# HGRN2 scan on one Trainium2 core: block totals kept at the blocks' first positions, and the epsilon of the norms added by ScalarE

## The chip, the cores and the metric

The kernel runs on one core of a Trainium2 chip. The metric is the device time of one execution in microseconds (us). The engines are TensorE (PE; its weight loads are a queue of their own, PEld), VectorE (DVE), ScalarE (ACT), GpSimd (POOL) and SyncE (SP, which issues most transfers).

## The reference

One layer of a decoder, everything float32, with T = 1024 positions and D = 1024 channels: an HGRN2 mixer of 8 heads of 128 channels, then an MLP of 4096 hidden channels, and a norm at the end. Cut to what is computed:

```
h = rmsnorm(x) * gain
q, f, i, g = split(h @ w_in, 4)                    # w_in: 1024 x 4096
log_f = log(lb + (1 - lb) * sigmoid(f));  k = (1 - lb) * sigmoid(-f);  q = silu(q) * 128**-0.5
# in each head:  S_t = diag(f_t) S_{t-1} + k_t v_t^T ;  o_t = S_t^T q_t     (v = i)
o = o * rsqrt(mean(o*o) + 1e-6) * out_norm * silu(g)
x = x + o @ w_out
x = x + relu(rmsnorm(x) @ w1)**2 @ w2
out = rmsnorm(x)
```

## The kernel before

Each float32 operand of a large product is split into a high part, which ACT copies (L162 for the weights of the input projection, L782 for the output projection), and a low part, which DVE makes by subtraction (L163, L783); each product is three passes on TensorE (L209 to L211). The input projection of a head is two "pairs", one for q and f, one for v and g, and each of them is computed from seven products of half-size blocks named a, b, s2, s1, s3, s4, d in place of eight. The weight sums that s1 to s4 need are made on DVE (L145, tiles raw). So w5s1, w5s3, w5s4 and so on are split operands of pair 5, whose products belong to head 2; pair 2h and pair 2h+1 belong to head h, and while they are computed the recurrence of head h-1 runs beside them.

The recurrence works by levels. Within a chunk of 128 positions, blocks of 1, 2, 4, 8, 16, 32 and 64 positions are joined in twos. At each size m, the scores between the odd block's q and the even block's k are one set of small matmuls; then the level is closed: carry_q multiplies the odd block's q by the total of f over the even block, carry_k multiplies the even block's k by the total of the odd block, and carry_f multiplies the two totals into the total of the joined block. All three are products on DVE (L392, L399, L405). The total of a block is a column of the tile f itself; before the change it stands at the block's last position (column m - 1).

The levels are spread over steps, which a list at the end of scan_units gives for each head:

- prefixes, before the matmuls: q times f, the level-1 product of q, and the tile qd, which holds q as the diagonal and sizes 1 and 2 see it.
- small: matmuls of k with qd (L568), then carry_k, carry_f of size 1 and all three of size 2, then prefixes_2, and eight masked copies of the scores into the tile Ac (L579 to L583).
- prefixes_2: the product of q at size 4 and the tile qe (L590, ACT; L594, ACT; L595, DVE), which holds q as sizes 4 and 8 see it.
- middle: matmuls of k with qe (L601), then carry_k and carry_f of size 4, all three of size 8, and three masked copies (L610).
- leaf(16): matmuls of k and q of size 16 (L619), the level's three products, a masked copy (L622), and four copies of ACT from Ac into AT (L626).
- big(32) and big(64): matmuls (L649), ACT's copies into AT (L652), the three products; at size 64 the total goes to the tile tot.
- kt, vt, kv: transposes of k and v and the states' updates (L664 to L693).
- o_unit: the output o (L706, L708), its sums of squares on ACT (L712), then rstd_of; z_unit: z = o times rs_z on ACT (L718); zt: z's transposes on TensorE (L755).

rstd_of makes 1/sqrt(ss + eps): an addition and a power with exponent -0.5, both on POOL (L114, L115). It is called for z of each head (128 x 8), for the eight row tiles of the norm ahead of the MLP (rs_n), and for rows of the final norm (rs_f).

The order on TensorE is written by hand: the steps are put into the projection's matmuls at fixed distances (SPACING, 1730 ns of matmul time). The order on DVE, ACT, POOL and SP is written by hand only at the start of the program and again from the output projection on; within the scan a scheduler chooses it, from the order of the code, the readiness of operands and the buffers.

Of the kernel before, what the change touches and what calls it, by code (L numbers as in the profile page):

```python
# [29 lines left out]
P = 128  # L30
# [19 lines left out]
def trunk(ctx: ExitStack, tc: tile.TileContext, x, gains, masks, gfin, w_in, w_out, w1, w2, out):  # L50
# [60 lines left out]

    def rstd_of(ss, eps, width, tag):
        r = pool.tile([P, width], F32, name=f"rs_{tag}", tag=f"rs{width}", bufs=8 if width == 1 else 2)
        nc.gpsimd.tensor_scalar(r, ss, eps, None, op0=ALU.add)  # L114
        nc.gpsimd.tensor_tensor(r, r, neghalf[:, :width], ALU.pow)  # L115
        return r

# [131 lines left out]
    with tc.tile_pool(name="scan", bufs=1) as sp:  # L249
# [137 lines left out]
        def carry_q(q, f, m):  # L387

            n = T // (2 * m)
            te = halves(f, m)[:, :, 0, m - 1:m]  # L390
            qo = halves(q, m)[:, :, 1, :]
            nc.vector.tensor_tensor(qo, qo, te.to_broadcast([P, n, m]), ALU.mult)  # L392

        def carry_k(k, f, m):

            n = T // (2 * m)
            to = halves(f, m)[:, :, 1, m - 1:m]
            ke = halves(k, m)[:, :, 0, :]
            nc.vector.tensor_tensor(ke, ke, to.to_broadcast([P, n, m]), ALU.mult)  # L399

        def carry_f(f, m):

            fv = halves(f, m)
            te, to = fv[:, :, 0, m - 1:m], fv[:, :, 1, m - 1:m]
            nc.vector.tensor_tensor(to, te, to, ALU.mult)  # L405

        shapes = {"q": ([P, T], 2), "qd": ([P, T // LEAF, 80], 1), "k": ([P, T], 1), "f": ([P, T], 1),
                  "vT": ([P, T], 1), "sg": ([P, T], 1)}
# [128 lines left out]
        def prefixes(tl):  # L537


            q, f, qd = tl["q"], tl["f"], tl["qd"]  # L540
            qb = q.rearrange("p (n l) -> p n l", l=LEAF)
            nc.vector.tensor_tensor(qb, qd[:, :, :LEAF], f.rearrange("p (n l) -> p n l", l=LEAF), ALU.mult)
            nc.scalar.activation(qd[:, :, 32:48], qb[:, :, 1::2], AF.Copy)
            carry_q(q, f, 1)
            q4 = q.rearrange("p (n b j) -> p n b j", b=8, j=4)
            f4 = f.rearrange("p (n b j) -> p n b j", b=8, j=4)
            x1 = qd[:, :, 48:64].rearrange("p n (b j) -> p n b j", j=2)
            x0 = qd[:, :, 64:80].rearrange("p n (b j) -> p n b j", j=2)
            nc.scalar.activation(x1, q4[:, :, :, 2:4], AF.Copy)
            nc.vector.tensor_tensor(x0, q4[:, :, :, 2:4], f4[:, :, :, 1:2].to_broadcast([P, 32, 8, 2]), ALU.mult)  # L550

        def scan_units(h, tl):

# [6 lines left out]
            def small():  # L560
                pss = []
                for g in range(2):
                    ps = psum.tile([P, 4, 80], F32, name=f"lv{h}_0_{g}", tag="s")
                    pss.append(ps)
                    for j in range(4):
                        for b in range(P // LEAF):
                            n = (4 * g + j) * 4 + b
                            nc.tensor.matmul(ps[b * LEAF:(b + 1) * LEAF, j, :], k[:, n * LEAF:(n + 1) * LEAF],  # L568
                                             tl["qd"][:, n, :], start=True, stop=True)
                carry_k(k, f, 1)  # L570
                carry_f(f, 1)
                carry(2)
                prefixes_2()
                m0, m1, m2, m3 = (mk[:, i:i + 1, :] for i in range(4))
                m2, m3 = (m.rearrange("p c (b j) -> p c b j", j=4) for m in (m2, m3))
                for g, ps in enumerate(pss):
                    ac = Ac[:, 4 * g:4 * g + 4, :]
                    a4 = ac.rearrange("p c (b j) -> p c b j", j=4)
                    nc.vector.copy_predicated(ac, m0.to_broadcast([P, 4, LEAF]), ps[:, :, :LEAF])  # L579
                    nc.vector.copy_predicated(ac[:, :, 1::2], m1[:, :, 1::2].to_broadcast([P, 4, 16]), ps[:, :, 32:48])  # L580
                    for i, mm in enumerate((m2, m3)):
                        pv = ps[:, :, 48 + 16 * i:64 + 16 * i].rearrange("p c (b j) -> p c b j", j=2)
                        nc.vector.copy_predicated(a4[:, :, :, 2:4], mm[:, :, :, 2:4].to_broadcast([P, 4, 8, 2]), pv)  # L583

            def prefixes_2():
# [6 lines left out]
                q16, f16 = (a.rearrange("p (n b j) -> p n b j", b=2, j=16) for a in (q, f))  # L592
                x1, x0 = (qe[:, :, c:c + 16].rearrange("p n (b j) -> p n b j", j=8) for c in (16, 32))
                nc.scalar.activation(x1, q16[:, :, :, 8:16], AF.Copy)  # L594
                nc.vector.tensor_tensor(x0, q16[:, :, :, 8:16], f16[:, :, :, 7:8].to_broadcast([P, 32, 2, 8]), ALU.mult)  # L595

            def middle():
                ps = psum.tile([P, NC, 48], F32, name=f"lv{h}_4", tag="s")
# [2 lines left out]
                    nc.tensor.matmul(ps[b * LEAF:(b + 1) * LEAF, c, :], k[:, n * LEAF:(n + 1) * LEAF],  # L601
                                     st["qe"][:, n, :48], start=True, stop=True)
                carry_k(k, f, 4)
                carry_f(f, 4)
                carry(8)
                for i, j, lo in ((4, 4, 0), (5, 8, 16), (6, 8, 32)):
                    odd = [a.rearrange("p c (b two j) -> p c b two j", two=2, j=j)[:, :, :, 1, :]
                           for a in (Ac, mk[:, i:i + 1, :])]
# [20 lines left out]
            def carry(m):  # L629

                carry_q(q, f, m)
                carry_k(k, f, m)
                if m == 64:
                    tot = st["tot"] = sp.tile([P, NC], F32, name=f"tot{h}", tag="tot", bufs=2)
                    fv = halves(f, m)
                    nc.vector.tensor_tensor(tot, fv[:, :, 0, m - 1], fv[:, :, 1, m - 1], ALU.mult)
                else:
                    carry_f(f, m)

# [743 lines left out]
```

## Time and profile before

| | |
|---|---|
| median of 3 runs | 1139.62 us (1139.31 to 1140.0) |
| the profiled execution | 1139.92 us |
| its span | 1138.1 us |
| TensorE busy | 1126.3 us, 99% of the span |
| VectorE busy | 831.2 us, 73% |
| ScalarE busy | 593.8 us, 52% |
| GpSimd busy | 40.6 us, 4% |

The span runs from the first to the last instruction of the profiled execution; 1.8 us of the execution's time lie outside it. The scan's eight heads lie between about 50 us and 470 us, some 51 us each; the output projection, the MLP and the final norm follow to 1131 us, and the last 7 us are the final rows' norm and their way out. In a row of a timeline the first number is the start, the second the time from the start to the end of the group of like instructions (xN is how many), and brackets name how long the engine was idle before and what ended that. On DVE and ACT, an instruction's row reaches a little into the next one's.

### The profile page before, as it was taken

To read this page: it belongs to the slowest core of one execution; us is meant where nothing else is said; L and a number is where in the kernel's file an instruction comes from. 1 tells how busy PE (TensorE), PEld (TensorE's weight loads), DVE (VectorE), ACT (ScalarE), POOL (GpSimd) and SP (SyncE) were. 2 spreads that over 40 slices of the span, in tenths; PEclk is the share of its full clock that TensorE was granted. 3 is DMA by queue.
4 is the path that set the end of the run, shared out by engine and by line. 5 is a ranking of instruction groups with operands and counts; after the bars stand their busy time and mean duration, and the time that the engine had idled before them with its cause. 6 is when DMAs were issued, how large, how long until landed. Compare 5 with 4: busy or idle time off the path is not lost.

```text
span 1138.1 us, 17625 instructions
## 1 busy us (share of the span) xinstructions
PE 1126.3 (99%) x7052; PEld 931.2 (82%) x7052; DVE 831.2 (73%) x1208; ACT 593.8 (52%) x1036; POOL 40.6 (4%) x68
## 2 busy tenths in 40 slices
PE   9999999999999999999999999999999999999997
PEld 7778888887878778888888888888888888888886
DVE  6897888878787889677855664565498755777674
ACT  7756556464645575456664544454553443323552
POOL 1000000000000000010000000000000000000011
PEclk9999999999999999999999999999999999999999
DMA  6113132312223176412244522452798635323331
GB/s 264 38 39 133 62 122 76 112 57 93 75 76 126 55 263 205 150 74 75 93 190 180 203 120 103 185 204 108 259 364 299 206 113 220 113 93 97 126 129 75
DMA packets 48466, 158.58 MB, mean 139 GB/s; under 512 B 5504, under 2 KB 5632, under 8 KB 48384
## 3 DMA queue, kind: packets, MB, share of 16 engines
q1 hardware_dynamic: 47520, 156.26, 38.4%
q8 instruction: 55, 0.90, 0.3%
q10 hardware_dynamic: 864, 1.20, 0.3%
q14 instruction: 27, 0.22, 0.1%
HBM read 109.99 MB, written 47.45 MB: 138 GB/s over the span
## 4 chain that ended last, share of the span: by engine, by line
PE 88%; DVE 5%; ACT 2%; DMA 2%; issue 1%; POOL 1%; POOLq 0%; ACTq 0%; DVEq 0%
PE m1X L210 5%; PE m1X L211 5%; PE m1X L209 5%; PE m2X L209 5%; PE m2X L211 5%; PE m2X L210 5%; PE pX L209 4%; PE pX L211 3%; PE pX L210 3%; PE m1Y L210 3%; PE m2Y L209 3%; PE m1Y L211 3%; PE m1Y L209 3%; PE m2Y L211 3%; PE m2Y L210 3%; PE pY L209 2%
## 5 line engine op out<-in xcount | busy, mean ns | idle before, releaser
L993 ACT ACTIVATE a<-ai 128x1024 fp32r<-128x1024 f32 x56 | 58.9, 1052 | 71.4 <-PE m2X L210 28.3
L994 DVE TENSOR_TENSOR a<-ai,a 128x1024 fp32r<-128x1024 f32 x56 | 68.3, 1219 | 11.1 <-ACT a L993 11.1
L1095 ACT ACTIVATE e<-e 128x1024 f32<-128x1024 f32 x24 | 25.5, 1062 | 72.5 <-DVE e L1142 72.5
L1172 DVE TENSOR_TENSOR acc<-acc,m2X 128x512 f32<-128x512 f32 x32 | 21.1, 685 | 34.3 <-PE m2X L211 34.2
L392 DVE TENSOR_TENSOR q<-q,f 128x512 f32<-128x512 f32 x56 | 38.4, 687 | 2.2 <-PE lv L649 2.2
L399 DVE TENSOR_TENSOR k<-k,f 128x512 f32<-128x512 f32 x56 | 38.3, 684 | 0.0
L1092 ACT ACTIVATE e<-e 128x1024 f32<-128x1024 f32 x32 | 34.0, 1062 | 1.0
L626 ACT ACTIVATE AT<-Ac 32x256 f32<-32x256 f32 x32 | 13.3, 415 | 35.3 <-DVE Ac L622 35.1
L145 DVE TENSOR_TENSOR raw<-raw,raw 128x512 f32<-128x512 f32 x42 | 29.0, 689 | 0.8
L718 ACT ACTIVATE z<-o,rs_z 128x128 f32<-128x128 f32 x64 | 17.4, 384 | 17.8 <-POOL rs_z L115 17.8
L1123 ACT ACTIVATE e<-m1X 128x512 f32<-128x512 f32 x30 | 16.9, 593 | 17.2 <-PE m1X L211 17.2
L706 PE MATMUL o<-v,AT 128*128 128x128 f32 x128 | 23.4, 275 | 0.0
L114 POOL TENSOR_SCALAR rs_f<-fs 128x1 f32<-128x1 f32 x4 | 2.1, 531 | 570.5 <-ACT ot L1176 570.5
L1172 DVE TENSOR_TENSOR acc<-acc,m2Y 128x512 f32<-128x512 f32 x16 | 10.8, 686 | 15.4 <-PE m2Y L211 14.7
L708 PE MATMUL o<-S,q 128*128 128x128 f32 x112 | 21.7, 275 | 0.0
L1142 DVE TENSOR_TENSOR e<-e,m1Y 128x512 f32<-128x512 f32 x16 | 10.9, 686 | 14.2 <-PE m1Y L211 14.2
L706 PEld LDWEIGHTS o<-v,AT 128*128 128x128 f32 x128 | 19.4, 191 | 0.6
L405 DVE TENSOR_TENSOR f<-f 128x512 f32<-128x512 f32 (+5 forms) x48 | 19.0, 396 | 0.1
L693 DVE SCALAR_TENSOR_TENSOR S<-S,tot,kv 128x128 f32<-128x128 f32 x48 | 16.7, 347 | 2.0
L114 POOL TENSOR_SCALAR rs_z<-zs 128x8 f32<-128x8 f32 x8 | 3.7, 458 | 390.1 <-ACT z L712 390.1
L708 PEld LDWEIGHTS o<-S,q 128*128 128x128 f32 x112 | 17.0, 192 | 0.0
L712 ACT ACTIVATE z<-o 128x128 f32<-128x128 f32 x64 | 16.7, 284 | 0.1
(1843 smaller groups left out, 3886.4 us busy)
## 6 DMA issues: line engine op xcount, KB each, us to landing
raw<-in_w_in SPq DMA_DIRECT2D x32, 512.0 KB, 3.6
ai<-adt SPq DMA_DIRECT2D x32, 512.0 KB, 4.4
adB<-e SPq DMA_DIRECT2D x24, 512.0 KB, 2.6
adt<-t SPq DMA_DIRECT2D x24, 512.0 KB, 4.3
ai<-adB SPq DMA_DIRECT2D x24, 512.0 KB, 4.5
izs<-sd SPq DMA_DIRECT2D x21, 256.0 KB, 3.3
x<-in_x SPq DMA_DIRECT2D x8, 512.0 KB, 7.1
xr<-in_x SPq DMA_DIRECT2D x8, 512.0 KB, 5.5
```

The costliest lines, as they stand in the source:

```text
L145: nc.vector.tensor_tensor(out_, a, b, ALU.add)
L209: nc.tensor.matmul(ps, lhi, rhi, start=start, stop=False, **more)
L210: nc.tensor.matmul(ps, lhi, rlo, start=False, stop=False, **more)
L211: nc.tensor.matmul(ps, llo, rhi, start=False, stop=stop, **more)
L392: nc.vector.tensor_tensor(qo, qo, te.to_broadcast([P, n, m]), ALU.mult)
L399: nc.vector.tensor_tensor(ke, ke, to.to_broadcast([P, n, m]), ALU.mult)
L706: nc.tensor.matmul(ps[:, j, :], AT[:, c, :], v[:, c, :], start=True, stop=c == 0)
L708: nc.tensor.matmul(ps[:, j, :], q[:, c * P:(c + 1) * P], st["S"][:, c - 1, :], start=False, stop=True)
L993: nc.scalar.activation(hi, x, AF.Copy)
L994: nc.vector.tensor_tensor(lo, x, hi.bitcast(F32), ALU.subtract)
L1092: nc.scalar.activation(t, t, AF.Square)
L1172: nc.vector.tensor_tensor(t, t, ps, op)
```

## The change

- **Where totals stand.** carry_f writes the joined total to the first position of the even block rather than the last of the odd one, and all readers take it from there. carry_k reads the odd block's total, which carry_f of the same size no longer overwrites; so carry_f of a size need not wait for carry_k of that size, nor carry_k of one size stand between the totals of this and the next.
- **What is written where.** carry_f(1), carry_q(2), carry_f(2) move from small, behind its matmuls, into prefixes, ahead of them. carry_f(4), carry_q(8), carry_f(8) move from middle into prefixes_2. In small and middle only carry_k remains.
- **Epsilon.** In rstd_of the addition is an ACT activation (Copy with a bias) instead of a POOL tensor_scalar. The power stays on POOL. There are 20 such additions: 8 for rs_z, 8 for rs_n, 4 for rs_f.

The diff (line numbers behind the additions shift by 3 to 4):

```diff
     def rstd_of(ss, eps, width, tag):
...
-        nc.gpsimd.tensor_scalar(r, ss, eps, None, op0=ALU.add)
+        nc.scalar.activation(r, ss, AF.Copy, bias=eps)
         nc.gpsimd.tensor_tensor(r, r, neghalf[:, :width], ALU.pow)
...
         def carry_q(q, f, m):
-            te = halves(f, m)[:, :, 0, m - 1:m]
+            te = halves(f, m)[:, :, 0, 0:1]
...
         def carry_k(k, f, m):
-            to = halves(f, m)[:, :, 1, m - 1:m]
+            to = halves(f, m)[:, :, 1, 0:1]
...
         def carry_f(f, m):
-            te, to = fv[:, :, 0, m - 1:m], fv[:, :, 1, m - 1:m]
-            nc.vector.tensor_tensor(to, te, to, ALU.mult)
+            te, to = fv[:, :, 0, 0:1], fv[:, :, 1, 0:1]
+            nc.vector.tensor_tensor(te, te, to, ALU.mult)
...
         def prefixes(tl):
...
+            carry_f(f, 1)
+            carry_q(q, f, 2)
+            carry_f(f, 2)
...
             def small():
...
                 carry_k(k, f, 1)
-                carry_f(f, 1)
-                carry(2)
+                carry_k(k, f, 2)
                 prefixes_2()
...
             def prefixes_2():
...
+                carry_f(f, 4)
+                carry_q(q, f, 8)
+                carry_f(f, 8)
...
             def middle():
...
                 carry_k(k, f, 4)
-                carry_f(f, 4)
-                carry(8)
+                carry_k(k, f, 8)
```

On TensorE the order is the same, instruction by instruction. What moves elsewhere is shown at three places of head 1.

VectorE, head 1, from k of size 1, behind the size-1 and size-2 matmuls, to qe. In the names, q1, k1, f1 are the head's tiles, lv1_0_0 and lv1_0_1 the matmuls' results, and the shape tells the size (128x256x2 is size 2). Before:

```order
L399 TENSOR_TENSOR k1_991<-k1_991,f1_992 128x512
L583 COPY_PREDICATED Ac_153<-mk_74,lv1_0_0_1249 128x32x2
L405 TENSOR_TENSOR f1_992<-f1_992 128x512
L579 COPY_PREDICATED Ac_153<-mk_74,lv1_0_1_1266 128x128
L392 TENSOR_TENSOR q1_825<-q1_825,f1_992 128x256x2
L399 TENSOR_TENSOR k1_991<-k1_991,f1_992 128x256x2
L580 COPY_PREDICATED Ac_153<-mk_74,lv1_0_1_1266 128x64
L405 TENSOR_TENSOR f1_992<-f1_992 128x256
L583 COPY_PREDICATED Ac_153<-mk_74,lv1_0_1_1266 128x32x2
L392 TENSOR_TENSOR q1_825<-q1_825,f1_992 128x128x4
L583 COPY_PREDICATED Ac_153<-mk_74,lv1_0_1_1266 128x32x2
L595 TENSOR_TENSOR qe1_1288<-q1_825,f1_992 128x32x16
```

The same place now, where f of size 1, q and f of size 2 stand ahead of the matmuls, and three of the masked copies behind qe (L597 now):

```order
L399 TENSOR_TENSOR k1_991<-k1_991,f1_992 128x512
L585 COPY_PREDICATED Ac_153<-mk_74,lv1_0_0_1252 128x32x2
L399 TENSOR_TENSOR k1_991<-k1_991,f1_992 128x256x2
L392 TENSOR_TENSOR q1_825<-q1_825,f1_992 128x128x4
L581 COPY_PREDICATED Ac_153<-mk_74,lv1_0_1_1269 128x128
L597 TENSOR_TENSOR qe1_1288<-q1_825,f1_992 128x32x16
L405 TENSOR_TENSOR f1_992<-f1_992 128x128
L582 COPY_PREDICATED Ac_153<-mk_74,lv1_0_1_1269 128x64
```

The stretch from the first k to qe has twelve rows before and six now; f of size 4 follows qe at once.

VectorE, head 1, from q of size 16 to k of size 32; raw50 and w5s1, w5s3 are weights of pair 5. Before:

```order
L392 TENSOR_TENSOR q1_825<-q1_825,f1_992 128x32x16
L399 TENSOR_TENSOR k1_991<-k1_991,f1_992 128x32x16
L622 COPY_PREDICATED Ac_153<-mk_74,lv1_16_1403 128x256
L405 TENSOR_TENSOR f1_992<-f1_992 128x32
L145 TENSOR_TENSOR raw50_1135<-raw50_1135 128x512
L145 TENSOR_TENSOR raw50_1135<-raw50_1135,raw51_1136 128x512
L392 TENSOR_TENSOR q1_825<-q1_825,f1_992 128x16x32
L399 TENSOR_TENSOR k1_991<-k1_991,f1_992 128x16x32
```

Now:

```order
L392 TENSOR_TENSOR q1_825<-q1_825,f1_992 128x32x16
L399 TENSOR_TENSOR k1_991<-k1_991,f1_992 128x32x16
L405 TENSOR_TENSOR f1_992<-f1_992 128x32
L626 COPY_PREDICATED Ac_153<-mk_74,lv1_16_1403 128x256
L163 TENSOR_TENSOR w5s1_1526<-raw50_1138,w5s1_1526 128x512
L145 TENSOR_TENSOR raw50_1138<-raw50_1138,raw51_1139 128x512
L163 TENSOR_TENSOR w5s3_1591<-raw50_1138,w5s3_1591 128x512
L392 TENSOR_TENSOR q1_825<-q1_825,f1_992 128x16x32
L399 TENSOR_TENSOR k1_991<-k1_991,f1_992 128x16x32
```

Between the masked copy into Ac and q of size 32 (128x16x32) there were two weight sums and a short product of f; now there are a sum and the splits of w5s1 and w5s3. In head 2 the order is the same with w7; in heads 3 to 6 q and k of size 32 stand ahead of the second split; in head 7 six splits of the output projection's operands stand ahead of q of size 32 where three did.

ScalarE, head 1, the same place; L626 before and L630 now are the four copies that the masked copy into Ac releases. Before:

```order
L162 ACTIVATE w5b_1454<-raw51_1136 128x512
L626 ACTIVATE AT_576<-Ac_153 32x8x32 x4
L519 ACTIVATE q2_1381<-pX4_1323 128x512
L162 ACTIVATE w5s1_1526<-raw50_1135 128x512
L162 ACTIVATE w5s3_1591<-raw50_1135 128x512
L652 ACTIVATE AT_576<-lv1_32_1471 32x4x32 x4
```

Now:

```order
L162 ACTIVATE w5b_1454<-raw51_1139 128x512
L162 ACTIVATE w5s1_1526<-raw50_1138 128x512
L630 ACTIVATE AT_576<-Ac_153 32x8x32 x4
L519 ACTIVATE q2_1381<-pX4_1326 128x512
L162 ACTIVATE w5s3_1591<-raw50_1138 128x512
L656 ACTIVATE AT_576<-lv1_32_1471 32x4x32 x4
```

The copy for w5s1 moved ahead of AT; the copy for w5s3 stays behind AT and the copy of q2.

## Rows read from the trace of the kernel before

**Rows 1.** Page, its first line: the span of the profiled execution:

```profile
span 1138.1 us, 17625 instructions
```

**Rows 2.** Windows, scan and then output projection and MLP; busy us of each engine (instructions):

```profile
50.00:470.00 420.00, 417.44 (x3849) 344.09 (x3848) 351.27 (x674) 242.88 (x586) 18.20 (x17) 1.00 0.31 104
470.00:1131.00 661.00, 661.00 (x2952) 547.76 (x2951) 439.08 (x460) 310.41 (x377) 15.85 (x34) 1.00 0.44 160
```

**Rows 3.** Waits of the weight loads at L601: us in total, times, longest:

```profile
PEld lv L601 <- ACT qe L594: 5.3, 8, 1.3
```

**Rows 4.** Timeline, weight loads of L601, heads 1, 6, 7: start, us, idle before:

```profile
120.01 0.61 PEld L601 LDWEIGHTS lv<-qe,k 128*32 128x32 f32 x50 [0.35 <-ACT qe L594]
373.71 0.61 PEld L601 LDWEIGHTS lv<-qe,k 128*32 128x32 f32 x48 [1.19 <-ACT qe L594]
427.21 0.60 PEld L601 LDWEIGHTS lv<-qe,k 128*32 128x32 f32 x49 [1.31 <-ACT qe L594]
```

**Rows 5.** Timeline, matmul queue: transposes of z in heads 1, 0, 3, 7; a projection:

```profile
155.19 0.71 PE L755 MATMUL zt<-ident,z 128*128 128x128 f32 x5
104.06 0.80 PE L755 MATMUL zt<-ident,z 128*128 128x128 f32 x5
256.27 0.71 PE L755 MATMUL zt<-ident,z 128*128 128x128 f32 x5
465.12 0.62 PE L755 MATMUL zt<-ident,z 128*128 128x128 f32 x4
416.40 0.50 PE L209 MATMUL pY<-h0B,w15s 128*128 128x512 f32 x1 [0.27 <-ACT e L526]
```

**Rows 6.** Timeline, VectorE, head 1: f of size 1, q and f of 2:

```profile
115.47 0.69 DVE L405 TENSOR_TENSOR f<-f 128x512 f32<-128x512 f32 x1
116.27 0.68 DVE L392 TENSOR_TENSOR q<-q,f 128x512 f32<-128x512 f32 x1
117.61 0.61 DVE L405 TENSOR_TENSOR f<-f 128x256 f32<-128x256 f32 x1
```

**Rows 7.** Timeline, GpSimd: epsilon and power in heads 1 and 3:

```profile
151.17 0.25 POOL L114 TENSOR_SCALAR rs_z<-zs 128x8 f32<-128x8 f32 x1 [48.13 <-ACT z L712]
151.50 1.92 POOL L115 TENSOR_TENSOR rs_z<-rs_z,neghalf 128x8 f32<-128x8 f32 x1
252.44 0.79 POOL L114 TENSOR_SCALAR rs_z<-zs 128x8 f32<-128x8 f32 x1 [48.29 <-ACT z L712]
253.31 1.66 POOL L115 TENSOR_TENSOR rs_z<-rs_z,neghalf 128x8 f32<-128x8 f32 x1
```

**Rows 8.** Timeline, ScalarE: a small addition; AT, q and w5s in head 1:

```profile
25.52 0.20 ACT L377 ACTIVATE lb<-lb 128x1 f32<-128x1 f32 x1
127.85 0.85 ACT L626 ACTIVATE AT<-Ac 32x256 f32<-32x256 f32 x2 [4.91 <-DVE Ac L622]
129.57 0.60 ACT L519 ACTIVATE q<-pX 128x512 f32<-128x512 f32 x1
130.19 0.63 ACT L162 ACTIVATE w5s<-raw 128x512 fp32r<-128x512 f32 x1
```

**Rows 9.** Timeline, VectorE: masked copy, q, k of size 32 (head 1); k, q (head 7):

```profile
127.38 0.43 DVE L622 COPY_PREDICATED Ac<-mk,lv 128x256 f32<-128x256 uint8 x1
129.96 0.69 DVE L392 TENSOR_TENSOR q<-q,f 128x512 f32<-128x512 f32 x1 [0.71 <-PE lv L649]
130.57 0.69 DVE L399 TENSOR_TENSOR k<-k,f 128x512 f32<-128x512 f32 x1
421.71 0.69 DVE L399 TENSOR_TENSOR k<-k,f 128x512 f32<-128x512 f32 x1
437.41 0.69 DVE L392 TENSOR_TENSOR q<-q,f 128x512 f32<-128x512 f32 x1
```

**Rows 10.** Timeline, matmul queue: size-64 matmuls in heads 1 and 7:

```profile
131.41 0.69 PE L649 MATMUL lv<-q,k 128*64 128x64 f32 x16
439.31 0.69 PE L649 MATMUL lv<-q,k 128*64 128x64 f32 x16
```

More of the change, by code (lines that the diff above doesn't have):

```diff
@@ L594, in prefixes_2 @@
                 nc.scalar.activation(x1, q16[:, :, :, 8:16], AF.Copy)
-                nc.vector.tensor_tensor(x0, q16[:, :, :, 8:16], f16[:, :, :, 7:8].to_broadcast([P, 32, 2, 8]), ALU.mult)
+                nc.vector.tensor_tensor(x0, q16[:, :, :, 8:16], f16[:, :, :, 4:5].to_broadcast([P, 32, 2, 8]), ALU.mult)
+                carry_f(f, 4)
+                carry_q(q, f, 8)
+                carry_f(f, 8)
             def middle():
@@ L635, in carry @@
                     fv = halves(f, m)
-                    nc.vector.tensor_tensor(tot, fv[:, :, 0, m - 1], fv[:, :, 1, m - 1], ALU.mult)
+                    nc.vector.tensor_tensor(tot, fv[:, :, 0, 0], fv[:, :, 1, 0], ALU.mult)
                 else:
```

## The prediction

> **What bounds the kernel now.** I read the busy shares by stretch first, then the waits of TensorE, then the order of instructions on the two engines that those waits name. The span of the profiled execution is 1138.1 us [rows 1], its time 1139.92 us, so 1.8 us lie outside the span. In the stretch from 470 us to 1131 us, the output projection and the MLP, TensorE (PE) is busy for 661.00 of 661.00 us; in the scan, from 50 us to 470 us, for 417.44 of 420.00 us [rows 2]. TensorE is thus the bound throughout, at the full granted clock of 1.00 in both, and its instructions stand in the same order in both kernels. So the change can move the end only through the moments in which TensorE stands still: in the stretch after 470 us there are none, and in the scan they are a few us together. The head start of 50 us and the tail of 7 us behind 1131 us hold nothing of the recurrence. VectorE (DVE), busy 351.27 of 420.00 us in the scan, ScalarE (ACT), 242.88, and GpSimd (POOL), 18.20 [rows 2], count only where TensorE waits for them.
>
> **Where TensorE waits.** The largest group with another engine's name behind it is the first weight load of the size-4 and size-8 matmuls (L601), which waits for qe: 5.3 us in 8 times, 1.3 us the longest [rows 3]. Even a prompt one shows 0.35 us, since that row stands in a head in which DVE was in time (its first row) [rows 4]. So 5.3 - 8 x 0.35 = 2.5 us are real, of which heads 6 and 7 hold 1.19 - 0.35 = 0.84 and 1.31 - 0.35 = 0.96 us [rows 4]. Next come the transposes of z (L755), whose duration holds the wait: eight take 1.03 us in a head without one, 1.57 in head 0, 1.29 in head 3, 1.65 in head 7, that is 0.54, 0.26 and 0.62 us more [rows 5]. Last, one projection matmul of head 7 waits 0.27 us for ACT's copy e [rows 5]. All this is 2.5 + 1.4 + 0.3 = 4.2 us, and no edit of this kind can win more.
>
> **Part 1: totals at first positions, q and f ahead.** Nothing is added or removed on DVE; the 32 products of f and 16 of q that move are the same work. Moved ahead of the small matmuls are f at size 1, q at size 2 and f at size 2; as DVE starts the next one about 0.09 us before the last row's end, they are worth 0.60 + 0.60 + 0.52 = 1.72 us of the chain that ended in qe [rows 6]. Three masked copies go behind qe as well. As 1.72 us is more than the longest real wait, 0.96, all of the **2.5 us** at L601 should go: what is late next there is TensorE itself. The three moved ones now run while the projection before them feeds TensorE. DVE has 420.00 - 351.27 = 69 us idle in the scan [rows 2], 8.6 us a head; if that cover is gone, 1.72 us a head come back on DVE, but in front of TensorE only where the size-1 matmuls wait for qd, and qd is written before two of the three. I take nothing for it.
>
> The ACT copy e in head 7 comes about half a us earlier, as one operand split now fills the idle time in which ACT waited for POOL: **0.3 us** gained (0 if not) [rows 5].
>
> **Part 2: epsilon on ACT.** Twenty additions leave POOL. In the scan POOL's take from 0.25 us (head 1) to 0.79 us (head 3), each with a power of 1.66 to 1.92 us behind it [rows 7]. The trace has no ACT addition of 128 x 8; the nearest ACT row is one of 128 x 1, 0.20 us [rows 8], the upper end POOL's own 0.79. I take 0.20, as ACT has just made the sums itself and nothing stands between. z, and with it the transposes, comes 0.05 to 0.6 us earlier: 0.1 of 0.54 us in head 0, whose addition is a short one, all 0.26 us in head 3. In head 7 ACT has its operand splits earlier too, so I take 0.55 of 0.62 us; if one of those splits, 0.58 us (half of 1.16, [rows 8]), is late and stands ahead of z, that turns into a loss of 0.58. Together **0.9 us** gained (from 0.2 lost to 1.2 gained). The twelve additions of the MLP's and the final norm lie beside a TensorE that is never idle [rows 2]; they are worth nothing, and 12 x 0.20 = 2.4 us at the very most if that cover were gone everywhere.
>
> **Part 3: what the scheduler's new order puts ahead of the size-64 matmuls.** This is the price. In head 1 the size-64 matmuls start at 131.41 us [rows 10]; they need q and k of size 32, and k of size 32 ends at 130.57 + 0.69 = 131.26 [rows 9]. TensorE follows 0.15 us behind, so there is no slack. In heads 1 and 2 the new order puts the split of w5s3 (w7s3) on DVE ahead of q of size 32. That split needs ACT's copy w5s3, which stands on ACT behind four copies AT and the projection's copy of q. When it is there: the masked copy that releases AT started at 127.38 before [rows 9]. From the stretch of DVE ahead of it a product of q, short ones of f and a split have left, and a split and two sums have come; the balance is small, I take 0.25 us earlier (0 to 0.75). AT then starts at 127.6 rather than 127.85, takes 1.72 us (to 129.57), q 0.60 and one split 0.58 [rows 8]: 127.6 + 1.72 + 0.60 + 0.58 = 130.50. DVE's split, q and k follow at 0.60, 0.61 and 0.69: 132.40. TensorE starts 0.15 us behind, at 132.55 instead of 131.41: **+1.1 us in each of two heads** (0.6 and 1.35 with the ends of the copy). On DVE itself q of size 32 waits, and behind it k, f and tot; nobody but TensorE waits for those.
>
> In head 7 six operand splits stand ahead of q of size 32 where three did. That stretch took 437.41 - 421.71 = 15.70 us [rows 9]; less 1.7 for what moved out (two products of f, one of q, a sum) and plus 3 x 0.60 = 1.80 for the splits it takes about 15.8, and starts 0 to 0.4 us earlier. q would start near 437.3, and k end 0.60 + 0.69 later, at 438.6, TensorE behind it at 438.75. TensorE, which has lost 0.96 + 0.27 us less by then, could be there at 439.31 - 1.2 = 438.1 [rows 10]: **+0.65 us** (0 to 1.1). Head 0 has one more split, 0.1 us. In heads 3 to 6 q of size 32 stands ahead of the second split; DVE idles 0.71 us ahead of it in head 1 [rows 9], and these heads need no more than that.
>
> **The sum.** Gains 2.5 + 0.3 + 0.9 = 3.7 us; prices 2 x 1.1 + 0.65 + 0.1 = 3.0 us. Net 0.7 us: 1139.92 - 0.7 = 1139.2 us against the profiled execution, which is 0.3 us above the median of 1139.62, so **1138.9 us**. With every term at its better end: gains 2.5 + 0.3 + 1.2 = 4.0, prices 2 x 0.6 = 1.2; 1136.8 us by the median. At its worse end: gains 2.5 + 0 - 0.2 = 2.3, prices 2 x 1.35 + 1.1 + 0.1 = 3.9, 1141.2 us. What a measurement of this kernel can tell from no change is about 0.2%, 2.3 us: most of this span lies within it.
>
> **The rivals.**
> (a) **The price does not come.** ACT might reach w5s3 in time, because the projection ahead of it is shorter of waits than I count. For it: DVE has 8.6 us of idle time a head. Against it: AT's 1.72 us stand ahead of w5s3 in ACT's new order. All gains stay: 1139.62 - 3.7 = 1135.9 us. Chance 0.17.
> (b) **Slower: the hold-up spreads.** In heads 3 to 6 the first split of the next pair (w9s1 and so on) and a sum now stand ahead of q of size 32, and the split needs ACT's copy. The point at which this decides: ACT more than 0.71 us late [rows 9]. If ACT then has AT's 1.70 us ahead of it [rows 8], each of four heads loses 1.0 us: 1138.9 + 4.0 = 1142.9 us. Against it: ACT's order has w9s1 ahead of AT. Chance 0.13.
> (c) **Nothing moves at all.** TensorE makes up what it waited for from work that would have waited later, since DVE's stream is the same in length: a wait taken from qe comes back at size 64. 1139.6 us. For it: 417.44 of 420.00 us are busy. Chance 0.12.
> (d) **POOL's power is held up.** Something held the addition in head 3, 0.79 instead of 0.25 us, and the power stays on POOL, now beside products of DVE that were elsewhere before. If one of these, 0.69 us, holds it in each head, z comes no earlier and part 2's 0.9 us are lost: 1139.8 us. Against it: the power took 1.66 us in head 3, whose addition was held, and 1.92 us in head 1, whose addition was not [rows 7]. Chance 0.06. The Trainium skill, page "SBUF — State Buffer", section "Who interferes with whom", states the rule that speaks for this rival: a DVE operation with two SBUF inputs and a GpSimd operation that reads SBUF take the same ports by turns, the later one waiting for the whole of the earlier. The spread of the addition agrees with it, the power's times do not show it.
>
> **How the numbers follow.** My forecast has 0.52; with (c) and (d) 0.70 lies inside 1136.8 to 1141.2. To leave out no more than 2 in 10, the range goes down to (a), 1135.8, and up to 1141.4, short of (b). Faster by over 2.3 us, under 1137.3: (a) and a little of the forecast's lower end, 0.20. Slower by over 2.3 us, above 1141.9: (b), 0.13. The rest, 0.67.
>
> **What would show it.** Right: the weight loads of L601 all at 0.35 us; z's transposes near 1.03 us in heads 3 and 7; a new wait of about a us at the size-64 matmuls of heads 1 and 2, with VectorE's q of size 32 behind the split w5s3, and one in head 7. Wrong: no wait at size 64 (then rival a), waits there in heads 3 to 6 (rival b), or a wait at the size-1 matmuls, which would mean that the moved products were not covered.

## The result: slower by 6.5 us, and the profile after

The changed kernel takes 1145.91 us (median of 6 runs, 1145.62 to 1146.92), the kernel before beside it 1139.46 us (6 runs): ratio 1.0057, 95% interval 1.0047 to 1.0068. The forecast was 1138.9 us, no difference. The profiled execution took 1146.54 us with a span of 1144.7 us, 6.6 us more than that of [rows 1]. Times of kernels here and below are medians; one execution of totals_only, below, took 2289.59 us, twice the others, and is left out.

The windows of the changed kernel (us, busy us of PE, PEld, DVE, ACT, POOL with instructions, granted clock, DMA share, GB/s):

```profile
50.00:470.00 420.00, 415.98 (x3816) 338.93 (x3815) 348.69 (x668) 240.79 (x581) 22.21 (x9) 1.00 0.31 104
470.00:1131.00 661.00, 661.00 (x2954) 547.75 (x2953) 440.73 (x462) 315.89 (x398) 10.92 (x21) 1.00 0.43 159
1131.00:1144.70 13.70, 7.35 (x39) 6.13 (x37) 3.72 (x6) 3.19 (x8) 1.67 (x5) 0.90 0.30 115
```

Against [rows 2], the granted clock is the same, the stretch from 470 us on is as full as before, and 7.35 us of TensorE's work have moved behind 1131 us. So the time was lost in the scan, where 33 matmuls fewer fit into the same 420 us. But TensorE's busy time fell by only 1.5 us there: most of the loss hides inside "busy" durations, and has to be read from single groups.

Waits of the weight loads, changed kernel (us in total, times, longest):

```profile
PEld lv L653 <- issue: 7.3, 14, 1.5
PEld lv L606 <- issue: 2.5, 7, 0.4
PEld lv L653 <- PE oY L211: 1.4, 1, 1.4
```

The matmuls behind qe (L606 now) wait no longer than an ordinary 0.35 us; the 5.3 us of [rows 3] are gone, as forecast. The matmuls of sizes 32 and 64 (L653 now) wait up to 1.5 us, as forecast too.

The matmul queue at z's transposes (L759 now), heads 0 to 7:

```profile
104.06 1.66 PE L759 MATMUL zt<-ident,z 128*128 128x128 f32 x8
156.50 2.12 PE L759 MATMUL zt<-ident,z 128*128 128x128 f32 x8
209.34 2.12 PE L759 MATMUL zt<-ident,z 128*128 128x128 f32 x8
261.02 2.11 PE L759 MATMUL zt<-ident,z 128*128 128x128 f32 x8
312.67 2.12 PE L759 MATMUL zt<-ident,z 128*128 128x128 f32 x8
364.35 2.11 PE L759 MATMUL zt<-ident,z 128*128 128x128 f32 x8
416.01 1.25 PE L759 MATMUL zt<-ident,z 128*128 128x128 f32 x8
472.36 1.03 PE L759 MATMUL zt<-ident,z 128*128 128x128 f32 x8
```

This was not forecast. The eight sum to 14.5 us; before they were 1.57, 1.29 and 1.65 us in heads 0, 3 and 7 and 1.03 us in five, 9.7 us ([rows 5] shows the first part of each of four groups). In heads 1 to 5 each transpose now follows ScalarE's next piece of z, so the group lasts as long as ScalarE's eight pieces of z, 2.17 us in head 3, and not TensorE's 1.03 us.

GpSimd, changed kernel, heads 0, 1, 3, 6 and 7, the power (the addition is ScalarE's now):

```profile
101.28 1.85 POOL L115 TENSOR_TENSOR rs_z<-rs_z,neghalf 128x8 f32<-128x8 f32 x1 [45.16 <-ACT rs_z L114]
152.66 3.37 POOL L115 TENSOR_TENSOR rs_z<-rs_z,neghalf 128x8 f32<-128x8 f32 x1 [49.54 <-ACT rs_z L114]
...
257.25 3.29 POOL L115 TENSOR_TENSOR rs_z<-rs_z,neghalf 128x8 f32<-128x8 f32 x1 [48.38 <-ACT rs_z L114]
...
412.85 1.82 POOL L115 TENSOR_TENSOR rs_z<-rs_z,neghalf 128x8 f32<-128x8 f32 x1 [48.97 <-ACT rs_z L114]
468.96 1.64 POOL L115 TENSOR_TENSOR rs_z<-rs_z,neghalf 128x8 f32<-128x8 f32 x1 [54.29 <-ACT rs_z L114]
```

The same power on the same 128 x 8 numbers took 1.66 to 1.92 us before [rows 7]. In heads 1 to 5 it takes 3.3 us. VectorE beside it, changed kernel, head 3:

```profile
256.63 0.69 DVE L145 TENSOR_TENSOR raw<-raw 128x512 f32<-128x512 f32 x1
257.23 0.68 DVE L392 TENSOR_TENSOR q<-q,f 128x512 f32<-128x512 f32 x1
257.83 0.68 DVE L145 TENSOR_TENSOR raw<-raw,raw 128x512 f32<-128x512 f32 x1
258.43 0.61 DVE L405 TENSOR_TENSOR f<-f 128x256 f32<-128x256 f32 x1
258.95 0.68 DVE L145 TENSOR_TENSOR vT<-vT,pZ 128x512 f32<-128x512 f32 x1
```

The power starts at 257.25 us, while q, a weight sum and f abut, all three with both inputs in SBUF. It ends at 257.25 + 3.29 = 260.54 us, which is 1.59 us after the addition to vT starts, and that one reads pZ from PSUM. In heads 1, 2, 4 and 5 the distance from vT's start is 1.59 to 1.60 us too. So the power seems to do nothing until the run of products ends. Before, the same place on VectorE in head 3 was idle for 0.62 us:

```profile
252.44 0.69 DVE L145 TENSOR_TENSOR raw<-raw,raw 128x512 f32<-128x512 f32 x1
253.75 0.69 DVE L145 TENSOR_TENSOR vT<-vT,pZ 128x512 f32<-128x512 f32 x1 [0.62 <-PE pZ L211]
```

**The balance**, in us against before, from these groups and, where a wait hides in a duration, from the lag of TensorE's instructions, that is, by how much later the same instruction starts in the changed kernel: z's transposes +4.9; size-64 matmuls +3.7 (heads 1 and 2, 1.17 each; head 7, 1.03; head 0, 0.38); size-16 matmuls and the states of head 7 +0.7; qe -2.5; the projection behind e -0.3. That is 6.5 of the 6.6 us.

### The profile page after: what moved, and what is told of

Same layout as the page of the kernel before. It is cut to its first block, busy times and chain, and to the rows that moved or that the text cites. A ratio compares the mean times of both kernels' runs of the same rounds, so it can differ in the third digit from the quotient of the medians.

```text
span 1144.7 us, 17612 instructions
## 1 busy us (share of the span) xinstructions
PE 1131.0 (99%) x7052; PEld 931.1 (81%) x7052; DVE 832.4 (73%) x1208; ACT 598.7 (52%) x1056; POOL 40.4 (4%) x48
## 4 chain that ended last, share of the span: by engine, by line
PE 86%; DVE 8%; ACT 3%; DMA 1%; issue 1%; POOL 1%; SPq 0%; DVEq 0%; ACTq 0%; POOLq 0%
PE m1X L209 5%; PE m1X L211 5%; PE m1X L210 5%; PE m2X L210 5%; PE m2X L211 5%; PE m2X L209 5%; PE pX L209 4%; PE pX L211 4%; PE pX L210 4%; PE m1Y L209 3%; PE m2Y L210 3%; PE m2Y L211 3%; PE m1Y L211 3%; PE m1Y L210 3%; PE m2Y L209 3%; PE pY L209 2%
## 5 line engine op out<-in xcount | busy, mean ns | idle before, releaser
L115 POOL TENSOR_TENSOR rs_z<-rs_z,neghalf 128x8 f32<-128x8 f32 x8 | 21.8, 2731 | 392.6 <-ACT rs_z L114 392.6
L115 POOL TENSOR_TENSOR rs_f<-rs_f,neghalf 128x1 f32<-128x1 f32 x4 | 2.7, 682 | 573.3 <-ACT rs_f L114 573.3
L630 ACT ACTIVATE AT<-Ac 32x256 f32<-32x256 f32 x32 | 13.3, 416 | 13.5 <-DVE Ac L626 13.2
L519 ACT ACTIVATE q<-pX 128x512 f32<-128x512 f32 x14 | 8.4, 599 | 16.7 <-PE pX L211 16.6
```

## Experiments

Theory A, from the above: VectorE's run of products holds GpSimd's power, z is late, and TensorE follows ScalarE through z. Theory B: the power is slow for a reason of its own, since ScalarE now writes its input and the addition no longer stands ahead of it on GpSimd. Line numbers below are those of each kernel, shifted by a few.

### Which part of the change

**totals_only** and **totals_only_2**: the changed kernel with one line back.

```diff
-        nc.scalar.activation(r, ss, AF.Copy, bias=eps)
+        nc.gpsimd.tensor_scalar(r, ss, eps, None, op0=ALU.add)
```

> The changed kernel with the epsilon added by GpSimd again; TensorE's order is the same and VectorE's differs in two neighbours of head 7. Theory A (VectorE's products of two SBUF tiles, run end to end since f1, q2 and f2 fill its idle gap, hold POOL's power): the power, or the addition ahead of it, is still held in heads 1 to 5, addition and power together over 3.3 us, z's transposes about 2.1 us there, time 1145.0 to 1147.5 us. Theory B (the power is slow because ScalarE writes its input, or because it is now POOL's first instruction after a long idle time): the power is back at 1.66 us, z's transposes at 1.03 us, time about 1141 us.

totals_only_2 is the same kernel once more, and the trace read below is of it.

> The kernel of totals_only once more, for a profile of an undisturbed execution: GpSimd adds the epsilon, everything else as changed. Theory A: addition and power together over 3.3 us in heads 1 to 5 (before: 1.9 to 2.5 us), z's transposes about 2.1 us there; 1148 to 1149.5 us as measured, which is 2 to 3 us over the changed kernel, since the addition can be held as well. Theory B would need the power at 1.66 us and z's transposes at 1.03 us.

Measured: 1148.95 us (1148.15 to 1149.54), then 1148.75 us (before beside it 1139.35; ratio 1.008, 1.006 to 1.010): 3 us worse than the whole change. GpSimd, totals_only_2, head 3:

```profile
258.14 2.19 POOL L114 TENSOR_SCALAR rs_z<-zs 128x8 f32<-128x8 f32 x1 [48.06 <-ACT z L716]
260.42 1.66 POOL L115 TENSOR_TENSOR rs_z<-rs_z,neghalf 128x8 f32<-128x8 f32 x1
```

The hold moved to the addition, which takes 0.25 us when free [rows 7]; the power behind it is free. z's transposes take 2.13 us in heads 1 to 5, where Theory B wanted 1.03. So whichever GpSimd instruction comes first is held, and Theory B falls. The epsilon on ScalarE is no cause of the loss; it saves one hold.

**eps_only**: the kernel before with the opposite edit, the addition on ScalarE.

> The kernel before with only the epsilon moved to ScalarE. Theory A: the power takes 1.66 to 2.0 us in all heads, z's transposes 1.03 us in heads 1, 2, 4 and 5; time 1138.9 to 1140.0 us, no difference to before. Theory B: the power takes 3.3 us in heads 1 to 5, z's transposes about 2 us, time about 1144 us.

Measured: 1138.86 us against 1139.55 (ratio 0.9998, 0.9989 to 1.0007), the power 1.64 to 1.98 us, head 3's transposes back from 1.29 to 1.03 us:

```profile
252.13 1.68 POOL L115 TENSOR_TENSOR rs_z<-rs_z,neghalf 128x8 f32<-128x8 f32 x1 [48.63 <-ACT rs_z L114]
```

No loss, as Theory A said. By the lag of TensorE's instructions the transposes gain 0.46, 0.26 and 0.62 us in heads 0, 3 and 7 and lose 0.37 us in head 6: the 0.9 us that part 2 of the prediction counted are there, but too small to be told from no change in the time.

### The mechanism

**gated**: the changed kernel, but f of size 1 has a factor of one that ScalarE makes from the last piece of z of the head before, so it and what follows from it cannot run beside the power.

```diff
+                one = gate[0] = pool.tile([P, 1], F32, name=f"one{h}", tag="ss", bufs=8)
+                nc.scalar.activation(one, st["z"][:, NC - 1, :1], AF.Copy, scale=0.0, bias=1.0)
...
-            carry_f(f, 1)
+                carry_f(f, 1, gate[0])
...
+                nc.vector.scalar_tensor_tensor(te, te, one, to, op0=ALU.mult, op1=ALU.mult)
```

> The changed kernel, but f of size 1 (and with it q and f of size 2) of a head waits for z of the head before, through a factor of one that ScalarE writes from z; so VectorE has its idle gap during POOL's power again. Theory A: the power is back at 1.66 to 2.0 us in heads 1 to 5, z's transposes at 1.03 us, the weight loads at qe stay at 0.35 us, and the waits of 1.2 us at the size-64 matmuls of heads 1 and 2 stay: 1145.9 - 5.0 = 1140.9 us, down to 1139.5 if head 7 loses less too. Theory B: the power stays at 3.3 us, time 1145.9 us.

Measured: 1145.07 us (1143.91 to 1146.29, 4 runs; ratio 1.0048, 1.0034 to 1.0061). GpSimd, then the matmul queue, head 3:

```profile
257.30 1.68 POOL L115 TENSOR_TENSOR rs_z<-rs_z,neghalf 128x8 f32<-128x8 f32 x1 [48.89 <-ACT rs_z L114]
```

```profile
261.07 1.03 PE L768 MATMUL zt<-ident,z 128*128 128x128 f32 x8
```

The power is as Theory A says in all heads (1.65 to 1.98 us), and the transposes in heads 0 to 5; in heads 6 and 7 they take 1.39 and 1.75 us. The time is not as it says, by 4 us (by 3 in the profiled execution, 1143.91 us, the shortest of the four): the waits at the matmuls of sizes 32 and 64 (L660 here) grew.

```profile
PEld lv L660 <- issue: 11.9, 16, 2.3
```

They were 7.3 + 1.4 + 0.7 us in the changed kernel, and 5.7 us before, which is the ordinary 0.36 us of 16. In head 1 the wait is now 2.24 us, where it was 1.51. So the run shows that the hold comes with the products' place beside the power, and not what the change costs without it: with the products later on VectorE, its masked copy, and ScalarE's copies AT behind it, come 1.5 us later in head 1, 0.8 of them by TensorE's own lag, and the wait for the split of w5s3 grows by the other 0.7.

**two_sbuf** and **one_psum**: the kernel before with three more VectorE instructions a head, which nobody needs, released by the last sum of squares. They differ in one operand.

```diff
+                for i in range(3):
+                    nc.vector.scalar_tensor_tensor(st["kt"][:, :4, :], v[:, 4:, :], ss[:, 7:8], v[:, :4, :],
+                                                   op0=ALU.mult, op1=ALU.mult)
```

In one_psum the last operand is st["o"][1], the output o in PSUM, in place of v[:, :4, :].

> The kernel before, with three more VectorE instructions a head that nobody needs, released by the last sum of squares, that is, as POOL begins: v times a sum times v, all in SBUF, written over a tile that is free by then. They stand ahead of the addition of pZ to vT. Theory A: the power is held until vT's addition starts (that one reads PSUM); addition and power together 3.3 to 4 us in heads 1 to 5, z's transposes about 2 us; 1139.5 + 5 = 1144.5 us (1143 to 1147). If VectorE's load alone were the cause, this run and its twin with a PSUM operand would come out the same.

> The twin of two_sbuf: the same three additional VectorE instructions at the same place (the third behind vT's addition), but the second tile is the output o, which lies in PSUM. Theory A: the power is not held, addition and power together under 2.5 us, z's transposes 1.03 us in heads 1, 2, 4 and 5; 1139 to 1141 us. If VectorE's load alone were the cause, it is as two_sbuf.

Measured: two_sbuf 1148.96 us (ratio 1.0079, 1.0062 to 1.0096), one_psum 1137.24 us (ratio 0.9979, 0.9970 to 0.9989). GpSimd in head 3 of two_sbuf, behind the additional instructions on VectorE:

```profile
256.58 2.33 DVE L715 SCALAR_TENSOR_TENSOR kt<-v,zs 128x512 f32<-128x512 f32 x3 [0.19 <-ACT z L712]
256.64 0.80 POOL L114 TENSOR_SCALAR rs_z<-zs 128x8 f32<-128x8 f32 x1 [49.16 <-ACT z L712]
257.52 2.12 POOL L115 TENSOR_TENSOR rs_z<-rs_z,neghalf 128x8 f32<-128x8 f32 x1
```

and of one_psum, where the third stands behind the addition to vT:

```profile
251.51 1.53 DVE L715 SCALAR_TENSOR_TENSOR kt<-v,zs,o 128x512 f32<-128x512 f32 x2 [0.19 <-ACT z L712]
251.57 0.24 POOL L114 TENSOR_SCALAR rs_z<-zs 128x8 f32<-128x8 f32 x1 [48.54 <-ACT z L712]
251.89 1.66 POOL L115 TENSOR_TENSOR rs_z<-rs_z,neghalf 128x8 f32<-128x8 f32 x1
```

The same instructions begin 0.06 us ahead of GpSimd's addition in both: with both tiles in SBUF GpSimd's two instructions take 2.92 us (2.46 to 2.94 in the eight heads), with one in PSUM 1.90 us (1.90 to 1.92). So VectorE's load is not the cause, the place of its operands is. The sizes were forecast less well: the hold is shorter than the 3.3 to 4 us expected, two_sbuf's time lies above its range of 1143 to 1147 us, and one_psum's below 1139 to 1141 us. The Trainium skill, page "SBUF — State Buffer", section "Who interferes with whom", states just this: a VectorE instruction with two SBUF inputs contends with a GpSimd instruction that reads SBUF, one with at most one SBUF input, outside VectorE's two-port modes, does not; both runs agree. The 11.7 us between the two runs are more than z's lateness, 1 us a head: ScalarE's splits stand behind z, VectorE's behind those, and qe behind them. The waits at qe show it, two_sbuf and one_psum:

```profile
PEld lv L601 <- ACT qe L594: 11.2, 8, 1.9
```

```profile
PEld lv L601 <- ACT qe L594: 5.0, 8, 2.1
```

one_psum beats the kernel before, although it does more: by the lag of TensorE's instructions its waits at qe are 1.2 us shorter in heads 4 to 6 (and 0.8 us longer in head 7), and z's transposes 0.5 us in head 0. The additional instructions moved VectorE's sums jkt and jS behind z's transposes; whether that is the reason was not tried.

**sbuf_run**: two_sbuf with four instructions of 128 x 384 that write four places.

```diff
+                for t in (st["kt"][:, :3, :], st["S"][:, :3, :], st["kt"][:, 3:6, :], st["S"][:, 3:6, :]):
+                    nc.vector.scalar_tensor_tensor(t, v[:, 5:, :], ss[:, 7:8], v[:, :3, :],
+                                                   op0=ALU.mult, op1=ALU.mult)
```

> Like two_sbuf, but four additional instructions of 128 x 384 (about the same work) that write four different places, so that none waits for the one ahead and they can abut, as the products of the changed kernel do; in two_sbuf all three wrote the same place, stood 0.75 us apart, and POOL came in after each. If POOL gets no turn within an abutting run, the addition lasts until vT's addition starts, near 2 us, with the power at 1.66 us behind it; time as two_sbuf or above, 1148 to 1152 us. If POOL comes in between any two, addition and power take about 0.6 and 2.0 us, below two_sbuf's 2.9 together.

Measured: 1145.45 us (ratio 1.0058, 1.0041 to 1.0075). They abut, 0.53 us apart, and still GpSimd came in after one of them each time, the second of the two forecasts:

```profile
255.27 0.66 POOL L114 TENSOR_SCALAR rs_z<-zs 128x8 f32<-128x8 f32 x1 [49.06 <-ACT z L712]
256.01 1.86 POOL L115 TENSOR_TENSOR rs_z<-rs_z,neghalf 128x8 f32<-128x8 f32 x1
```

So abutting alone does not shut GpSimd out for a whole run. Between TENSOR_TENSOR products it got no turn in three of them (heads 1 to 5 of the changed kernel, all five alike), and in totals_only_2 in the rest of one and three more; between SCALAR_TENSOR_TENSOR ones it got one after each. In head 0 of the changed kernel it did get in between two TENSOR_TENSORs (power 1.85 us). What opens a turn is left open.

### The way to TensorE

**late_zt**: the changed kernel with z's transposes one step later in the list of steps.

```diff
-            return (([None] * 4 + [small] + [None] * 2 if h == 0 else [None] * 2 + [small, None, None]) + [middle, None, leaf(16, 7), None]
-                    + [big(32), big(64), None, kt, ("values", h), vt, kv, None, o_unit, lambda: (z_unit(), sums_load()), None, zt, sums_make])
+            return (([None] * 4 + [small] + [None] * 2 if h == 0 else [None] + [small, None, None]) + [middle, None, leaf(16, 7), None]
+                    + [big(32), big(64), None, kt, ("values", h), vt, kv, None, o_unit, lambda: (z_unit(), sums_load()), None, None, zt, sums_make])
```

> The changed kernel with z's transposes one step later on TensorE (1.73 us of other matmuls between z and them; the recurrence's next small matmuls stay where they are). VectorE's order ahead of the transposes is that of the changed kernel, so POOL's power stays held at 3.3 us in heads 1 to 5. Theory A (the held power reaches TensorE through z's transposes alone): they take 0.9 to 1.1 us in all heads, 5 us come back: 1145.9 - 5.0 = 1140.9 us (1140 to 1142), with the waits at the size-64 matmuls left. Rival: the late z also holds ScalarE's splits behind it, and with them TensorE elsewhere: 1144 us or more.

Measured: 1142.67 us (1140.90 to 1145.48, 6 runs; ratio 1.0029, 1.0017 to 1.0041), the profiled execution 1140.90 us. GpSimd, then the matmul queue, head 3:

```profile
255.07 3.29 POOL L115 TENSOR_TENSOR rs_z<-rs_z,neghalf 128x8 f32<-128x8 f32 x1 [47.28 <-ACT rs_z L114]
```

```profile
260.88 1.03 PE L759 MATMUL zt<-ident,z 128*128 128x128 f32 x8
```

The power is held as in the changed kernel, and the transposes do not wait, in all heads. So TensorE waits for the held power through the transposes. How much time that gives back is less sure. By the medians it is 3.2 us, and 1142.67 us lies between the two forecasts. The profiled execution is the shortest of the six, so that it meets the 1140.9 us forecast is luck: in its trace the transposes gain 6.2 us, since those of heads 0 and 6 gain too, and waits elsewhere take 0.6 us back. The executions scatter by 4.6 us; in the three longest the mean granted clock is 0.995 to 0.997, in the three shortest 0.998 to 0.999. Where it fell in them no trace shows; before_late_zt below has such a place in its own.

**hold_split**: the changed kernel; VectorE's splits of w5s3 and w7s3 get a factor of one that VectorE makes from k of size 32 of heads 1 and 2.

```diff
+                    if m == 32:
+                        one = held[2 * h + 3] = pool.tile([P, 1], F32, name=f"held{h}", tag="ss", bufs=8)
+                        nc.vector.tensor_scalar(one, k[:, :1], 0.0, 1.0, op0=ALU.mult, op1=ALU.add)
...
+            if m == "s3" and n in (5, 7):
+                nc.vector.scalar_tensor_tensor(w[:, 1], src, held[n], w[:, 0].bitcast(F32), op0=ALU.mult, op1=ALU.subtract)
```

> The changed kernel, but VectorE's splits of w5s3 and w7s3 wait for k of size 32 of heads 1 and 2 (through a factor of one that VectorE makes from that k), so they no longer stand ahead of it. If those splits cause the waits at the size-64 matmuls of heads 1 and 2, the waits of 1.2 us each go and the rest stays: 1145.9 - 2.3 = 1143.6 us. If VectorE is simply late there, they stay or come back in the next step: 1145 to 1146 us.

Measured: 1145.14 us (ratio 1.0048, 1.0033 to 1.0063), 1.5 us above the forecast for the splits as cause, and where the rival put it. The trace decides between the two. At the size-64 matmuls of head 1 the wait is ordinary (it was 1.51 us in the changed kernel):

```profile
131.92 0.55 PEld L657 LDWEIGHTS lv<-q,k 128*64 128x64 f32 x16 [0.37 <-issue]
```

Both waits, 2.35 us, are gone and did not come back in the next step, so the splits cause them. The time shows only 0.8 us of it, since the new order gave much of it back elsewhere: in head 0 the power is held now too (3.20 us) and costs 0.5 us at the transposes, and in head 7 the states wait 0.6 us longer and the transposes 0.8 us.

### Towards a better version

**mixed**: the gate of gated, with the totals at first positions in heads 3 to 7 only.

```diff
+        NEW = 3
+        def at(m):
+            return m - 1 if head[0] < NEW else 0
...
-            te = halves(f, m)[:, :, 0, 0:1]
+            te = halves(f, m)[:, :, 0, at(m):at(m) + 1]
```

> Totals at the last positions and the old order of steps in heads 0 to 2 (which hardly waited at qe), totals at the first positions with the gate in heads 3 to 7; epsilon on ScalarE. VectorE's order in heads 0 to 2 is that of before. Theory A: no wait at the size-64 matmuls of heads 1 and 2, z's transposes at 1.03 us, no waits at qe in heads 4 to 7 (2.35 us): 1139.5 - 2.35 = 1137.1 us, up to 1138.5 with a wait left in head 7. Theory B: 1143 us or more, since the power would be held in heads 1 to 5.

Measured: 1139.10 us against 1139.55 (11 runs; ratio 0.9994, 0.9985 to 1.0003): no difference, and above the 1137.1 to 1138.5 us forecast. The waits at qe and in heads 1 and 2 are gone as forecast; 0.55 us came back at the size-32 matmuls of head 6, 0.42 us at the size-64 matmuls of head 7 (the expectation of mixed_late_zt below puts both at size 64), 0.1 to 0.2 us at size 16 in heads 4 to 7, and 0.4 us at the transposes of head 6.

**before_late_zt**: the kernel before with the transposes one step later.

> The kernel before with z's transposes one step later, nothing else. Theory A: only the 1.4 us that they waited in heads 0, 3 and 7 come back: 1138.1 us. Rival: the later transposes make products behind them late, 1139.5 us or more.

The edit is that of late_zt. Measured: 1138.25 us against 1139.59 (11 runs; ratio 0.9991, 0.9982 to 1.0000), as forecast, at the edge of what can be told. But three of the eleven executions took 1139.61 to 1140.17 us and the other eight 1137.48 to 1138.39 us, and the profiled one, the longest of all, shows the rival: in head 7 the weight load behind qe waits 2.74 us, where it waited 1.31 us before [rows 4], and for 2.80 us behind it TensorE's granted clock is 0.50, the lower of its two levels, 1.2 GHz:

```profile
426.53 0.89 PEld L601 LDWEIGHTS lv<-qe,k 128*32 128x32 f32 x64 [2.74 <-ACT qe L594]
```

```profile
427.50:430.30 2.80, 2.80 (x14) 2.19 (x8) 2.67 (x8) 1.63 (x3) 0.00 (x0) 0.50 0.91 320
```

By the lag of TensorE's instructions this place costs 2.95 us against before: 1.43 in the wait, since ScalarE's copy for qe stands behind a copy that waits for z's transfer, and the rest in the matmuls behind it, which follow each other at 0.43 us instead of 0.23. Whether the two other long executions lost their time there too, no trace shows.

**mixed_late_zt**: both, with first positions in heads 4 to 7 only.

```diff
-        NEW = 3
+        NEW = 4
```

> Meant as the better version: totals at first positions and the gate in heads 4 to 7 alone (where qe was waited for: 2.35 us), the old ones in heads 0 to 3, epsilon on ScalarE, z's transposes one step later. Theory A: 1139.5 - 2.35 - 1.4 = 1135.8 us, up to 1137.5 with the waits of 0.4 to 0.55 us at the size-64 matmuls of heads 6 and 7 that mixed had. Rival: waits come back at the next step, 1138.5 us or more.

Measured: 1137.55 us against 1139.59 (11 runs, 1136.96 to 1137.86; ratio 0.9981, 0.9972 to 0.9990). It beats both kernels, the one before by 2.0 us and the changed one by 8, at the upper end of the forecast: the waits at qe are ordinary in heads 4 to 7 and the transposes take 1.03 us. In the scan TensorE is busy for 418.75 of 420.00 us, against 417.44 [rows 2]:

```profile
50.00:470.00 420.00, 418.75 (x3861) 346.01 (x3860) 353.58 (x677) 245.83 (x604) 15.28 (x9) 1.00 0.32 105
```

## Why the prediction was wrong, point by point

- **The bound, and where TensorE waits: right.** All of the loss lies in the scan, in moments in which TensorE waits; nothing moved from 470 us on. But "no edit of this kind can win more" than 4.2 us said nothing of how much one can lose, and the reading of z's transposes stopped too early. 1.03 us is rightly read as "a head without one", that is, without a wait; how near the wait is was not asked. In head 1 before, ScalarE makes z from 153.46 us on, and the transposes start at 155.19 us [rows 5], before the last of the eight pieces is there:

```profile
153.46 2.18 ACT L718 ACTIVATE z<-o,rs_z 128x128 f32<-128x128 f32 x8 [2.37 <-POOL rs_z L115]
```

  The last piece ends at 155.64 us and the last transpose is due some 0.3 us later. There was almost no slack. In head 1 of the changed kernel z starts at 156.07 us and the transposes at 156.50 us (the rows of the transposes above), so z is 1.3 us later against TensorE, and 1.09 us of that are lost. Heads 2, 4 and 5 lose as much, head 3, which waited before, 0.82 us.
- **Part 1, qe: right in mechanism and size.** 2.5 us were forecast and 2.5 us came. The 0.3 us at ScalarE's copy e came too, through the split that now fills ScalarE's wait for GpSimd, but they are the epsilon's and not the totals': eps_only has them (0.36 us), totals_only_2 has not.
- **Part 1, "I take nothing for it": the step that failed.** The cover for the three moved products was counted as VectorE's 69 us of idle time in the scan, and the only way from them to TensorE was said to be the size-1 matmuls through qd. Those gaps were not free: in most heads GpSimd's power began in the gap ahead of vT's addition. q and f of size 2 fill it; the power is held 1.6 us, z is late, and TensorE loses 4.9 us at z's transposes. gated shows that it is their place beside the power, and two_sbuf against one_psum, with other products, that two SBUF operands hold GpSimd and one does not. What the prediction called cover was another engine's turn.
- **Part 2, the epsilon: right by itself, and wrong in the sum.** The addition took 0.21 us on ScalarE, and eps_only shows the gain at the transposes. In the changed kernel 0.9 us of gain were forecast at z's transposes and 4.9 us of loss came; only head 7's gain, 0.62 us, is there.
- **Rival (d) was what happened, mis-sized and given 0.06.** It had the mechanism: the power held by a moved product. It priced it at one product, 0.69 us, and let that only cancel a gain. The rows: 1.6 us in five heads, the rest of a run of products, with no slack behind it. Its evidence against, a power of 1.66 us in head 3 next to an addition that was held, was read wrongly: VectorE was idle during that power's first 0.4 us, so the row could not speak against a hold.
- **Part 3, the size-64 matmuls: right.** Heads 1 and 2 were forecast at 1.1 us each and measured 1.17; the steps were right one by one, as VectorE and ScalarE of the changed kernel show in head 1 (masked copy forecast at 127.13, split w5s3 at 130.50, TensorE at 132.55):

```profile
127.15 0.44 DVE L626 COPY_PREDICATED Ac<-mk,lv 128x256 f32<-128x256 uint8 x1
...
130.63 0.69 DVE L163 TENSOR_TENSOR w5s<-raw,w5s 128x512 fp32r<-128x512 f32 x1 [1.75 <-ACT w5s L162]
131.24 0.68 DVE L392 TENSOR_TENSOR q<-q,f 128x512 f32<-128x512 f32 x1
131.84 0.69 DVE L399 TENSOR_TENSOR k<-k,f 128x512 f32<-128x512 f32 x1
```

```profile
127.62 1.70 ACT L630 ACTIVATE AT<-Ac 32x256 f32<-32x256 f32 x4 [1.00 <-DVE Ac L626]
129.35 0.60 ACT L519 ACTIVATE q<-pX 128x512 f32<-128x512 f32 x1
129.97 0.63 ACT L162 ACTIVATE w5s<-raw 128x512 fp32r<-128x512 f32 x1
```

```profile
132.68 0.69 PE L653 MATMUL lv<-q,k 128*64 128x64 f32 x16 [1.10 <-DVE f L405]
```

  Head 7 lost 1.03 us there rather than 0.65, head 0 0.38 rather than 0.1. hold_split shows the splits as the cause in heads 1 and 2.
- **The slower rival (b)** put the hold-up in heads 3 to 6 at the size-64 matmuls. It did not come there.
- **The range** ended at 1141.4 us, since all that was unknown was bounded one term at a time, from terms whose places were right. The cost that was missing stood on an engine with 4% of busy time.

## What to carry to other kernels

An idle gap of VectorE is no free cover until it is known who else uses it: ask of every product that moves which GpSimd instruction it will now stand beside, and whether both its inputs lie in SBUF. Ask of a chain that is in time by how much it is in time, for a consumer that follows its producer piece by piece shows no wait until the slack is gone. And an order that is made by a scheduler from readiness moves with dependencies, not with the place in the code: in this kernel VectorE's work that became ready earlier drew weight splits forward, and these, needed much later, stood ahead of q and k that TensorE was waiting for.

## What the runs showed of the hardware

- A GpSimd instruction that reads SBUF can be kept waiting by more than one VectorE instruction: a power of 1.66 us lasted 3.29 us beside a run of three abutting TENSOR_TENSORs with two SBUF inputs, and began to move when the next one read PSUM. The Trainium skill's page "SBUF — State Buffer", section "Who interferes with whom", states that the ports VectorE and GpSimd share are an exclusive lock; here the loser waited for three instructions one behind the other, in five heads of eight, while beside SCALAR_TENSOR_TENSORs it was one at a time.
- The wait does not show as idle time of GpSimd. It stands in the duration of the held instruction, so a busy share hides it, and one row's duration is to be read against the same row in other heads.
- A wait of TensorE can cost more than its length: behind one of 2.74 us in before_late_zt the granted clock was 0.50 for 2.80 us, and 1.5 us more were lost.
